# A two-layer hybrid encoder step on one core: a weight loaded two steps ahead, layer 1's parameters tied to their place, four units' weight splits moved to VectorE, and the barrier norms written in one piece

## The chip, the cores and the metric

One core of a Trainium2 chip runs the whole program. The time is the device time of one execution in microseconds (us); the kernel before takes 2740.53 us, the median of three runs (2738.47 to 2742.73). Engines are named as in the profile: PE is TensorE, DVE is VectorE, ACT is ScalarE, POOL is GpSimd, SP is the queue that issues nearly all DMAs. Each engine works off its own instructions in a fixed order and waits on semaphores.

## The reference, cut to what matters

512 prompt frames and 8 x 16 sample frames (640 columns in all) go through two layers of width 1024. Each layer computes `h = rmsnorm(x)`, `u = h @ w_in`, three branches from the columns of `u` (a convolution module, latent attention, a Mamba-2 SSD), `mix = (sum of sigmoid(gate_i) * branch_i @ w_mix_out[i]) @ w_out`, and then

```
x = x + rmsnorm(mix, g_post_mix)
f = rmsnorm(x, g_pre_ffn) @ w_gate_up
f = (silu(f[:, :D_FF]) * f[:, D_FF:]) @ w_down
x = x + rmsnorm(f, g_post_ffn)
```

So at two places in a layer (behind `w_out` and behind `w_down`) a norm of what was just computed, the residual sum and a second norm stand between one row of matmuls and the next. In the attention branch the sample frames' queries are multiplied by a transposed part of the key projection, here called `w_ukt`, before they meet the cached latents.

## The kernel before, in words

All activations lie transposed: 128 channels on the partitions, the 640 columns along the row, cut into half 0 (columns 0 to 255) and half 1 (256 to 639), `HALF`. A `Unit` is 128 output channels of one weight matrix. Its weights come in granules of four 128 x 128 blocks: `load_gran` brings one from memory on SP (tile `raw`, 4 buffers), ACT rounds it to `wh`, and DVE or POOL subtracts to get the rest, `wl` (`split`; the engine is an argument of the unit). Activations are split the same way (`hh` and `hl` for the normed input). `mm3` then does three matmuls per block: wh*hh, wh*hl, wl*hh. Products go to the tile `pg`, in PSUM, with 4 buffers, and `evac` takes them out on ACT and DVE.

The program is written by one loop at the end of `emit`, over a list of actions: run a unit's half A, run its half B, or call a hook. Loads are written three actions ahead of use (`loads[done:pos[i] + 3]`). After each half, `pump` advances side tasks: Python generators in lanes, each with a rate in steps per half. A `yield` in a task is a pause: what follows it is written at a later pump, among later matmuls. The lanes `bar` and `bar2` carry the norms, with about one step after each half of a unit with eight blocks; the lane `attn` carries attention. After this a planner (the framework's scheduler, `schedule_with_timeline_sim=True`) orders the instructions of each engine by when it believes their inputs to be there, earlier-written ones first. An instruction whose inputs it takes to be early can so be moved far ahead of where it was written.

A barrier (`barrier`, `add_halves`) is where half 0 of the next stage needs the norm of half 0 of this one. All units of the old stage run their half 0, then all of them half 1; meanwhile the norm of half 0 is advanced in lane `bar`. Then the new stage's first 12 units run half 0 (here called the A stretch), during which the norm of half 1 is advanced in lane `bar2`, and then half 1 (the B stretch). The norms are flushed where they are needed. `postnorm` (L424) sums squares over the channels with a matmul (`cs`), loads the old residual from memory (`xl`, eight DMAs), takes the root on DVE (`rsqrt`, nine short instructions, result `ry`), spreads it with a matmul (`rb`), and on DVE scales (`mo` or `dn`, eight) and adds the residual (eight); then it squares on ACT and sums on DVE (`psq`, seven adds), and stores. `prenorm` (L396) does `cs`, `rsqrt`, `rb`, scales into `ht` (eight on DVE) and splits into `hh` (ACT) and `hl` (eight on DVE). `bar_mix` (L1312) and `bar_ffn` (L1352) chain the two. The start of the kernel does the same with `first_norm`, and the end of the last layer with `bar_ffn` without `prenorm`.

`load_params` (L361) loads a layer's small parameters `pk` with a DMA on ACT's queue and derives `an` (ACT, then DVE) and `hp` (three on DVE). Layer 1's is written at the barrier between the layers. `wu` makes the units of `w_in`; in both layers POOL does their weight subtraction. In the first A and B stretch of a layer nine of the twelve units are loaded twice, once for each half; krdt, kv0, kv1 and q0 are the first four of them. `task_attn` (L621) begins with the loads of `qn` and then, four times: load `w_ukt` (`al`, 128 KB), pause, eight matmuls into `qlp`, copy, store. Convolution taps are long series of DVE instructions (`cv`) and POOL adds.

Of the kernel before, what the change touches and what calls it, by code (L numbers as in the profile page):

```python
# [13 lines left out]
AF = mybir.ActivationFunctionType  # L14
ALU = mybir.AluOpType
AX = mybir.AxisListType

D_MODEL, SEQ, DEPTH, NB, DS, PAST = 1024, 512, 2, 8, 16, 256
# [39 lines left out]
WIN_IDX = {n: i for i, n in enumerate(WIN_UNITS)}  # L58
# [13 lines left out]
BY = 2  # L72
# [4 lines left out]
def emit(tc, ctx, I, O):  # L77
    nc = tc.nc
    dma = nc.sync.dma_start
    act = nc.scalar.activation  # L80
    V, G = nc.vector, nc.gpsimd
# [16 lines left out]
    def nm(s):  # L98
        uid[0] += 1
        return f"{s}_{uid[0]}"  # L100

    def blk(shape, s="b", dt=F32):
        return bpool.tile(shape, dt, tag="b", name=nm(s))

    def hf(w, s="h", dt=F32):
        return hpool.tile([P, w], dt, tag="hf", name=nm(s))
# [7 lines left out]
    def tiny(shape, s="t", dt=F32):  # L114
        return tpool.tile(shape, dt, tag="t", name=nm(s))

    def psb(shape, s="pb"):
        return psb_.tile(shape, F32, tag="pb", name=nm(s))

    def mm(ps, l, r, a, b):  # L120
        nc.tensor.matmul(ps, l, r, start=a, stop=b)  # L121
# [14 lines left out]
    def tt(eng, o, a, b, op):  # L136
        eng.tensor_tensor(o, a, b, op=op)  # L137

    def stt(o, a, s, b, op0, op1):
        return V.scalar_tensor_tensor(o, a, s, b, op0=op0, op1=op1)  # L140
# [10 lines left out]
    def split(hi, lo, src, eng=None):  # L151
        nc.scalar.copy(hi, src)  # L152
        tt(eng or V, lo, src, hi.bitcast(F32), ALU.subtract)
# [30 lines left out]
    def colsum(sq, n):  # L184

        ps = psb([P, 24], "cs")
        for j in range(n):
            mm(ps[:, j:j + 1], sq[:, j * P:(j + 1) * P], C["ones"], True, True)
        return ps

    def rsqrt(ps, n, scale, post=1.0):

        v, q = ps[:, 8:8 + n], ps[:, 16:16 + n]
        s, r, t, y = (tiny([P, 8], x)[:, :n] for x in ("rs", "rr", "rt", "ry"))
        a = V.tensor_scalar(v, ps[:, :n], scale / post ** 2, EPS / post ** 2, op0=ALU.mult, op1=ALU.add)
        for i in tap.values():
            tc.add_manual_dep(a.ins, i.ins.name, behind)
        V.tensor_scalar(s.bitcast(I32), v.bitcast(I32), 0.5, float(0x1fbb4f2e), op0=ALU.mult, op1=ALU.add)
        V.reciprocal(r, s)
        tt(V, q, v, r, ALU.mult)  # L200
        tt(V, t, q, s, ALU.add)
        V.reciprocal(r, t)
        tt(V, q, v, r, ALU.mult)
        stt(t, t, 0.25 * HERON ** 2, q, ALU.mult, ALU.add)
        root.append(V.reciprocal(y, t))
        return y

    def bcast(y, n):
        rb = psb([P, n * P], "rb")
        for j in range(n):  # L210
            mm(rb[:, j * P:(j + 1) * P], y[:, j:j + 1].broadcast_to([P, P]), C["ident2"], True, True)
        return rb
# [144 lines left out]
    def layer(l):  # L357
# [4 lines left out]
        def load_params():  # L362
            pk = lpool.tile([P, NPK], F32, tag="pk", bufs=2, name=nm("pk"))
            nc.scalar.dma_start(pk, I["pk"][l])
            L["pk"] = pk
            an = lpool.tile([P, 16], F32, tag="an", bufs=2, name=nm("an"))
            o = _PK["a_log"][0]
            act(an, pk[:, o:o + 16], AF.Exp)
            V.tensor_scalar(an, an, -1.0, None, op0=ALU.mult)
            L["aneg"] = an  # L370
            hp = lpool.tile([P, 16], F32, tag="hp", bufs=2, name=nm("hp"))
            for j, n in enumerate(("conv_ln_g", "conv_ln_b")):
                o = _PK[n][0]
                V.tensor_scalar(hp[:, 4 * j:4 * j + 4], pk[:, o:o + 4], 0.5, None, op0=ALU.mult)
            o = _PK["d_skip"][0]
            V.tensor_scalar(hp[:, 8:16], pk[:, o:o + 8], 0.5, None, op0=ALU.mult)
            L["hp"] = hp

        def par(n, j):
            o = _PK[n][0]  # L380
            return L["pk"][:, o + j:o + j + 1]


        def new_h():
            L["h"] = [tuple(blk([P, NT], t, F32R) for t in ("hh", "hl")) for _ in range(8)]
# [4 lines left out]
        def squares(xs, half):  # L390
            r = [hf(HW[half], "psq") for _ in range(8)]
            for k in range(8):
                act(r[k], xs[k][:, HALF[half]], AF.Square)
            for a, b in ((0, 1), (2, 3), (4, 5), (6, 7), (0, 2), (4, 6), (0, 4)):
                tt(V, r[a], r[a], r[b], ALU.add)
            return r[0]  # L396

        def prenorm(xs, sq, half, gname, ps=None):
            c, w, n = HALF[half], HW[half], HCH[half]
            if ps is None:  # L400
                ps = colsum(sq, n)
            yield
            y = rsqrt(ps, n, 1.0 / D_MODEL)
            yield
            rb = bcast(y, n)
            for k in range(8):
                tmp = hf(w, "ht")
                stt(tmp, xs[k][:, c], par(gname, k), rb, ALU.mult, ALU.mult)
                hh, hl = L["h"][k]
                split(hh[:, c], hl[:, c], tmp)  # L410
            yield
# [12 lines left out]
        def postnorm(key, tiles, half, gname, src, dst, sq=True):  # L424

            c, n, w = HALF[half], HCH[half], HW[half]
            yield
            ps = colsum(L.pop(("sq", key, half)), n)
            xs = []
            for k in range(8):  # L430
                xs.append(hf(w, "xl"))
                dma(xs[k], src[k][:, c])
            yield
            rb = bcast(rsqrt(ps, n, 1.0 / D_MODEL), n)
            for k in range(8):
                t = tiles[k][:, c]
                stt(t, t, par(gname, k), rb, ALU.mult, ALU.mult)
                tt(V, t, t, xs[k], ALU.add)
            r = squares(tiles, half) if sq else None
            for k in range(8):  # L440
                dma(dst[k][:, c], tiles[k][:, c])
            for _ in range(BY):
                yield
            return r


        win = I["w_in"][l]

        def wu(name, evac, done=None):
            return Unit(win[WIN_IDX[name]], 8, h_rhs, evac, done, G)  # L450


        def ev_krdt(ps, half, c):
# [166 lines left out]
        def al(src, w, rows=P, view=None):  # L620
            t = blk([rows, w], "al") if w > 384 else hf(w, "al")[:rows]  # L621
            dma(t if view is None else view(t), src)
            return t
# [7 lines left out]
        def task_attn():  # L631
# [51 lines left out]
            for i in range(2):  # L683
                a = blk([P, 512], "qn")
                dma(a[:64].rearrange("p (h n) -> p h n", h=4), qd[4 * i:4 * i + 4, :64, SEQ:].rearrange("h p n -> p h n"))
                r.append(a)
            yield
            for ct in range(2):
                for i in range(2):
                    w = al(I["w_ukt"][l, ct, :, i * 512:(i + 1) * 512], 512, 64)  # L690
                    yield
                    ps = psb([P, 4, P], "qlp")
                    for h in range(4):
                        c = slice(h * P, (h + 1) * P)
                        mm(ps[:, h, :], w[:, c], r[i][:64, c], True, True)
                    t = blk([P, NB, 4, DS], "qlt")
                    nc.scalar.copy(t, ps.rearrange("p h (b t) -> p b h t", t=DS))
                    dma(qld[ct][:, :, i * 64:(i + 1) * 64], t.rearrange("p b h t -> p b (h t)"))
# [135 lines left out]
            for hh in range(2):  # L834
# [4 lines left out]
                for p, w in zip((2 * hh, 2 * hh + 1), uv):  # L839
                    ps = psb([P, 256], "oss")  # L840
                    o = (p % 2) * 256
# [470 lines left out]
        def bar_mix(half):  # L1312
            sq = yield from postnorm("mo", L["mo"], half, "g_post_mix", xin, xd)
            if half == 0:
                new_h()
            yield
            yield from prenorm(L["mo"], sq, half, "g_pre_ffn")


# [34 lines left out]
        def bar_ffn(half):  # L1354
            sq = yield from postnorm("dn", L["dn"], half, "g_post_ffn", xd, O["y"] if last else xd, not last)
            if not last:
                nxt = layers[l + 1]
                if half == 0:
                    nxt["load_params"]()
                    nxt["new_h"]()  # L1360
                yield
                yield from nxt["prenorm"](L["dn"], sq, half, "g_pre_mix")

        def start():
            load_params()
            new_h()
# [22 lines left out]
        def schedule():  # L1389
# [9 lines left out]
            def glu(j):  # L1399
                return [wu(f"glu{j}a", ev_glu_a(j)), wu(f"glu{j}b", ev_glu_b(j), done_glu(j))]  # L1400
# [51 lines left out]
    done = 0  # L1452
# [3 lines left out]
    for i, (k, u, half) in enumerate(actions):  # L1456
# [3 lines left out]
        if i in pos:  # L1460
            for n in loads[done:pos[i] + 3]:
                actions[n][1].load()
            done = max(done, pos[i] + 3)
# [163 lines left out]
```

## Time and profile before

| | |
|---|---|
| median of 3 runs | 2740.53 us (2738.47 to 2742.73) |
| profiled execution: time, span | 2738.25 us, 2736.4 us |
| busy: PE, DVE, ACT, POOL | 2647.6, 1557.0, 1092.8, 810.7 us |
| PE clock granted, mean | 0.988 of full speed |

The busy shares are over the whole span. The stages are different: in the projection and attention stages DVE, ACT and POOL all have much to do, in the feed-forward stages nearly only PE. Where PE has an idle gap, the profile names what ended it; the clock of a stretch is in the view of windows.

### The profile page before, as it was taken

Reading aid. Unit: us, or ns where it says so; the run is one execution under the profiler, and the core shown is the slowest. Engines: PE = TensorE matmul, PEld = TensorE weight load, DVE = VectorE, ACT = ScalarE, POOL = GpSimd, SP = SyncE. Lnnn points to the kernel's source line nnn. Section 1 sums busy time; section 2 is a strip of 40 time slices with the busy share of each in tenths; the row PEclk is TensorE's granted clock in tenths of the full one; section 3 lists DMA queues with packets and bytes.
Section 4 is the critical chain, followed back from the end, with each engine's and each line's share of the span. In section 5 each row is a group of like instructions: output and inputs, shape, how many; then the busy total and the mean of one; then the engine's idle time right before and its main releaser. Section 6 shows DMA issues by size and latency. Waiting matters only on the chain. (4 is left out here: it accounts for less than half of the span.)

```text
span 2736.4 us, 47467 instructions
## 1 busy us (share of the span) xinstructions
PE 2647.6 (97%) x17652; PEld 2556.6 (93%) x17652; DVE 1557.0 (57%) x3382; ACT 1092.8 (40%) x2437; POOL 810.7 (30%) x796
## 2 busy tenths in 40 slices
PE   7999999999999899999999899999999998999997
PEld 7999898889999899999999898989999998999997
DVE  6364759576566632333665648677656666323336
ACT  5535454434325432222445354544433344322222
POOL 5554555554420000000156544645544200000000
PEclk9999999999999999999999999999999999999999
DMA  6453244543734432222454432453436443222224
GB/s 185 147 159 102 75 135 111 156 131 119 239 121 137 149 93 74 70 82 72 139 166 158 129 98 87 128 143 120 145 110 230 133 159 120 86 77 70 78 74 131
DMA packets 248536, 337.81 MB, mean 123 GB/s; under 512 B 52464, under 2 KB 139056, under 8 KB 248304
## 3 DMA queue, kind: packets, MB, share of 16 engines
q1 hardware_dynamic: 246720, 333.75, 39.2%
q8 instruction: 139, 2.28, 0.3%
q10 hardware_dynamic: 1584, 1.02, 0.1%
q14 instruction: 93, 0.76, 0.1%
HBM read 268.73 MB, written 65.94 MB: 122 GB/s over the span
## 5 line engine op out<-in xcount | busy, mean ns | idle before, releaser
L121 PE MATMUL pg<-hh,wh 128*128 128x256 f32 (+1 forms) x3296 | 1048.4, 319 | 25.6 <-DVE fg L140 18.2
L121 PE MATMUL pg<-hl,wh 128*128 128x256 f32 (+1 forms) x3296 | 1035.1, 314 | 4.6 <-DVE hl L137 4.6
L121 PE MATMUL pg<-hh,wl 128*128 128x256 f32 (+1 forms) x3296 | 1029.2, 313 | 0.0
L137 POOL TENSOR_TENSOR wl<-raw,wh 128x512 fp32r<-128x512 f32 (+2 forms) x364 | 506.8, 1398 | 1158.5 <-ACT wh L152 1106.3
L152 ACT CAST wh<-raw 128x512 fp32r<-128x512 f32 (+1 forms) x696 | 423.7, 610 | 846.7 <-PE pg L121 737.9
L121 PEld LDWEIGHTS pg<-hh,wh 128*128 128x128 f32 x3296 | 627.3, 190 | 37.7 <-DVE fg L140 18.6
L121 PEld LDWEIGHTS pg<-hl,wh 128*128 128x128 f32 x3296 | 627.6, 191 | 13.8 <-DVE hl L137 5.3
L121 PEld LDWEIGHTS pg<-hh,wl 128*128 128x128 f32 x3296 | 627.0, 190 | 5.6 <-issue 3.9
L137 DVE TENSOR_TENSOR wl<-raw,wh 128x512 fp32r<-128x512 f32 x332 | 224.3, 677 | 338.6 <-ACT wh L152 337.0
L121 PE MATMUL pg<-fh,wh 128*128 128x256 f32 (+1 forms) x648 | 200.6, 310 | 0.0
L121 PE MATMUL pg<-fl,wh 128*128 128x256 f32 (+1 forms) x648 | 200.1, 309 | 0.0
L121 PE MATMUL pg<-fh,wl 128*128 128x256 f32 (+1 forms) x648 | 200.0, 309 | 0.0
L140 DVE SCALAR_TENSOR_TENSOR cv<-pp,pk,cv 128x512 f32<-128x512 f32 x184 | 158.8, 863 | 2.7 <-POOL cv L137 2.7
L121 PEld LDWEIGHTS pg<-fh,wh 128*128 128x128 f32 x648 | 122.0, 188 | 0.0
L121 PEld LDWEIGHTS pg<-fl,wh 128*128 128x128 f32 x648 | 122.0, 188 | 0.0
L121 PEld LDWEIGHTS pg<-fh,wl 128*128 128x128 f32 x648 | 121.9, 188 | 0.0
L140 DVE SCALAR_TENSOR_TENSOR sa<-pd,pk,sa 128x664 f32<-128x664 f32 x96 | 106.6, 1110 | 16.9 <-ACT sa L996 16.3
L137 POOL TENSOR_TENSOR cv<-cv,cvt 128x640 f32<-128x640 f32 x56 | 89.8, 1603 | 74.4 <-ACT cvt L907 66.2
L140 DVE SCALAR_TENSOR_TENSOR cv<-sp,pk,cv 128x128 f32<-128x128 f32 x184 | 94.8, 515 | 0.0
L137 DVE TENSOR_TENSOR fg<-fg,pg 128x256 f32<-128x256 f32 (+1 forms) x88 | 42.6, 486 | 83.5 <-PE pg L121 83.2
L152 ACT CAST fh<-fg 128x256 fp32r<-128x256 f32 (+1 forms) x88 | 40.3, 460 | 111.3 <-DVE fg L137 108.3
L137 DVE TENSOR_TENSOR acc<-acc,sq 128x256 f32<-128x256 f32 (+1 forms) x96 | 59.8, 625 | 37.4 <-ACT sq L421 35.9
(307 smaller groups left out, 4411.7 us busy)
## 6 DMA issues: line engine op xcount, KB each, us to landing
raw<-in_w_in SPq DMA_DIRECT2D x284, 256.0 KB, 2.9
raw<-in_w_gu SPq DMA_DIRECT2D x208, 256.0 KB, 2.7
raw<-in_w_down SPq DMA_DIRECT2D x72, 256.0 KB, 2.7
raw<-in_w_mix SPq DMA_DIRECT2D x64, 256.0 KB, 3.0
ma<-gd SPq DMA_DIRECT2D x48, 320.0 KB, 4.7
raw<-in_w_out SPq DMA_DIRECT2D x48, 256.0 KB, 2.7
gd<-gs SPq DMA_DIRECT2D x48, 192.0 KB, 2.2
hb<-in_state_ssm SPq DMA_DIRECT2D x64, 128.0 KB, 3.2
```

The lines of the kernel that those rows point to most:

```text
L121: nc.tensor.matmul(ps, l, r, start=a, stop=b)
L137: eng.tensor_tensor(o, a, b, op=op)
L140: return V.scalar_tensor_tensor(o, a, s, b, op0=op0, op1=op1)
L152: nc.scalar.copy(hi, src)
```

## The change: what it does

It changes five things. (1) `w_ukt`: the first load is written with the `qn` loads, and in each step the load for the next step but one; at any time up to two are ahead. (2) Layer 1's `an` and `hp` instructions (four on ACT and DVE) may not be moved ahead of the instruction that was written before them on their engine; their DMA may. (3) In layer 0 the weight subtraction of krdt, kv0, kv1 and q0 goes to DVE in place of POOL. (4) `prenorm` loses both its inner pauses, `postnorm` one inner pause and one of two (`BY` = 2) at its end. (5) `bar_mix` and `bar_ffn` lose the pause between the two norms.

```diff
-            act(an, pk[:, o:o + 16], AF.Exp)
+            a = act(an, pk[:, o:o + 16], AF.Exp)
+            if l:
+                tc.keep_in_program_order(a)
...
-            V.tensor_scalar(hp[:, 8:16], pk[:, o:o + 8], 0.5, None, op0=ALU.mult)
+            a = V.tensor_scalar(hp[:, 8:16], pk[:, o:o + 8], 0.5, None, op0=ALU.mult)
+            if l:
+                tc.keep_in_program_order(a)
...
-            yield
-            y = rsqrt(ps, n, 1.0 / D_MODEL)
-            yield
-            rb = bcast(y, n)
+            rb = bcast(rsqrt(ps, n, 1.0 / D_MODEL), n)
...
                 dma(xs[k], src[k][:, c])
-            yield
             rb = bcast(rsqrt(ps, n, 1.0 / D_MODEL), n)
...
-            for _ in range(BY):
-                yield
+            yield
             return r
...
-            return Unit(win[WIN_IDX[name]], 8, h_rhs, evac, done, G)
+            eng = None if l == 0 and name in ("krdt", "kv0", "kv1", "q0") else G
+            return Unit(win[WIN_IDX[name]], 8, h_rhs, evac, done, eng)
...
+            def ukt_load():
+                if len(ukt) < 4:
+                    ct, i = parts[len(ukt)]
+                    ukt.append(al(I["w_ukt"][l, ct, :, i * 512:(i + 1) * 512], 512, 64))
+
+            ukt_load()
             yield
             for ct in range(2):
                 for i in range(2):
-                    w = al(I["w_ukt"][l, ct, :, i * 512:(i + 1) * 512], 512, 64)
+                    ukt_load()
+                    w = ukt[2 * ct + i]
                     yield
...
             if half == 0:
                 new_h()
-            yield
             yield from prenorm(L["mo"], sq, half, "g_pre_ffn")
...
                     nxt["new_h"]()
-                yield
                 yield from nxt["prenorm"](L["dn"], sq, half, "g_pre_mix")
```

A unit whose engine is `None` is split on DVE.

## Rows read from the trace of the kernel before

**Rows 1.** The page, part 1: busy us, share of the span, instructions.
```profile
PE 2647.6 (97%) x17652; PEld 2556.6 (93%) x17652; DVE 1557.0 (57%) x3382; ACT 1092.8 (40%) x2437; POOL 810.7 (30%) x796
```

**Rows 2.** Waits of PE: who waited for whom, us in total, times, longest.
```profile
PE pg L121 <- DVE fg L140: 18.2, 2, 9.1
PE qlp L121 <- DMA al<-in_w_ukt: 8.7, 3, 6.2
PE rb L121 <- DVE ry L205: 8.2, 3, 3.8
...
PE pg L121 <- DVE hl L137: 4.6, 3, 1.7
```

**Rows 3.** Timeline, `w_ukt` in layer 0: start, us, engine, operation, [idle before <- releaser].
```profile
166.38 0.56 SPq L622 DMA_DIRECT2D al<-in_w_ukt  x1
169.87 2.07 PE L121 MATMUL qlp<-qn,al 64*128 64x128 f32 x8 [2.20 <-DMA al<-in_w_ukt]
```

**Rows 4.** Windows: stretch, its us, busy us by engine, PEclk (granted), DMA share, GB/s.
```profile
169.87:177.00 7.13, 7.13 (x25) 6.90 (x26) 7.13 (x15) 1.21 (x2) 0.46 (x1) 0.53 0.23 66
1536.14:1543.00 6.86, 6.86 (x26) 6.63 (x27) 2.73 (x3) 2.04 (x3) 0.59 (x4) 0.58 0.61 184
...
1364.00:1376.00 12.00, 9.59 (x48) 9.30 (x49) 7.70 (x27) 3.77 (x9) 0.47 (x2) 0.57 0.50 158
...
846.00:880.00 34.00, 34.00 (x202) 34.00 (x201) 21.65 (x61) 15.24 (x35) 0.00 (x0) 1.00 0.42 131
880.00:930.00 50.00, 39.46 (x315) 39.05 (x314) 41.87 (x101) 24.39 (x51) 0.00 (x0) 0.90 0.51 169
```

**Rows 5.** Timeline, `w_ukt` in layer 1, on POOL, SP and PE.
```profile
1516.94 14.36 POOL L137 TENSOR_TENSOR wl<-raw,wh 128x512 fp32r<-128x512 f32 x1 [4.14 <-ACT wh L152]
...
1518.67 0.61 SPq L622 DMA_DIRECT2D al<-in_w_ukt  x1
1531.33 1.60 SPq L220 DMA_DIRECT2D raw<-in_w_in  x2
...
1521.50 1.16 PE L121 MATMUL qlp<-qn,al 64*128 64x128 f32 x8 [0.23 <-DMA al<-in_w_ukt]
...
1536.14 2.04 PE L121 MATMUL qlp<-qn,al 64*128 64x128 f32 x8 [6.25 <-DMA al<-in_w_ukt]
```

**Rows 6.** Waits of SP's queue from 1500 to 1545 us.
```profile
SPq L220 <- POOL wl L137: 17.5, 4, 11.7
```

**Rows 7.** Timeline at the `w_out` barrier of layer 0, on DVE and PE.
```profile
881.62 1.42 DVE L137 TENSOR_TENSOR hl<-ht,hh 128x256 fp32r<-128x256 f32 x4
...
896.14 4.29 DVE L140 SCALAR_TENSOR_TENSOR mo<-mo,pk,rb 128x384 f32<-128x384 f32 x8 [1.91 <-PE rb L121]
...
908.99 0.74 DVE L140 SCALAR_TENSOR_TENSOR fg<-ft,pg 128x256 f32<-128x256 f32 x2
...
927.14 3.36 DVE L137 TENSOR_TENSOR hl<-ht,hh 128x384 fp32r<-128x384 f32 x7
...
909.45 0.58 PE L121 MATMUL pg<-hh,wh 128*128 128x256 f32 x1 [9.08 <-DVE fg L140]
```

**Rows 8.** Timeline of PE at the barrier between the layers.
```profile
1364.71 1.19 PE L121 MATMUL rb<-c_ident,ry 128*128 128x128 f32 x4 [2.45 <-DVE ry L205]
...
1391.92 0.58 PE L121 MATMUL pg<-hh,wh 128*128 128x256 f32 x1 [2.37 <-ACT sq L421]
```

**Rows 9.** Timeline of the start, on DVE, ACT and PE.
```profile
13.50 0.29 DVE L374 TENSOR_SCALAR hp<-pk 128x4 f32<-128x4 f32 x2 [1.66 <-DMA pk<-in_pk]
...
19.95 0.62 ACT L152 CAST wh<-raw 128x512 fp32r<-128x512 f32 x1 [1.95 <-DMA raw<-in_w_in]
...
20.62 0.58 PE L121 MATMUL pg<-hh,wh 128*128 128x256 f32 x1 [3.16 <-ACT wh L152]
```

**Rows 10.** The page, part 5: weight subtractions, busy, mean ns of one, idle before.
```profile
L137 POOL TENSOR_TENSOR wl<-raw,wh 128x512 fp32r<-128x512 f32 (+2 forms) x364 | 506.8, 1398 | 1158.5 <-ACT wh L152 1106.3
...
L137 DVE TENSOR_TENSOR wl<-raw,wh 128x512 fp32r<-128x512 f32 x332 | 224.3, 677 | 338.6 <-ACT wh L152 337.0
```

More of the change, by code (lines that the diff above doesn't have):

```diff
@@ L373, in load_params @@
                 o = _PK[n][0]
-                V.tensor_scalar(hp[:, 4 * j:4 * j + 4], pk[:, o:o + 4], 0.5, None, op0=ALU.mult)
+                a = V.tensor_scalar(hp[:, 4 * j:4 * j + 4], pk[:, o:o + 4], 0.5, None, op0=ALU.mult)
+                if l:
+                    tc.keep_in_program_order(a)
             o = _PK["d_skip"][0]
-            V.tensor_scalar(hp[:, 8:16], pk[:, o:o + 8], 0.5, None, op0=ALU.mult)
+            a = V.tensor_scalar(hp[:, 8:16], pk[:, o:o + 8], 0.5, None, op0=ALU.mult)
+            if l:
+                tc.keep_in_program_order(a)
             L["hp"] = hp
@@ L686, in task_attn @@
                 r.append(a)
+            parts = [(ct, i) for ct in range(2) for i in range(2)]
+            ukt = []
+            def ukt_load():
[3 more added lines that the diff above has]
+            ukt_load()
             yield
```

## The prediction

> **What bounds the kernel now.** I read the page's first part, then PE's waits, then for each large wait the timeline of the engines around it, and last the windows for the granted clock. PE is busy 2647.6 of 2736.4 us [rows 1], so the gap to a kernel that never stops PE is 88.8 us, and a saving counts where it lies in such a gap, or where the gap leaves PE slow. Four lines of PE's waits belong to what the change touches [rows 2]: 18.2 us in two waits at the two `w_out` barriers, 8.7 in three for `w_ukt`, 8.2 in three for the root `ry`, 4.6 in three for `hl`. Together 39.7, nearly half of the gap. The clock adds to it: after the 2.20 us wait in layer 0 [rows 3] the stretch of 7.13 us shows 0.53 of full speed, so its first part ran at 1.2 in place of 2.4 GHz [rows 4]. All sums are made against the profiled execution, 2738.25 us (span 2736.4 and 1.85 around it). The median of the runs is 2.3 higher, and I add that at the end.
>
> **`w_ukt` two steps ahead.** Layer 0: the load is issued at 166.38, PE stands still until 169.87 for 2.20 [rows 3], then computes 7.13 us at 0.53. The same work at full speed takes 7.13 x 0.53 = 3.78, so the slow clock costs 3.35. Layer 1: a first wait of 0.23, then 6.25 [rows 5], then 6.86 us at 0.58, which costs 2.9 [rows 4]. Why so long: one `wl` on POOL took 14.36 us while DVE ran convolution taps, two of SP's next `raw` loads waited for the buffers it held (SP lost up to 11.7 us in one wait [rows 6]), and the second `w_ukt` load stood behind them in SP's queue; the first, at 1518.67, had got through before [rows 5]. With the change the second load is written where the first was, so it is ahead of the blocked pair. Both price items go: 2.20 + 3.35 + 0.23 + 6.25 + 2.9 = 14.9. What is late next: the half unit behind the stalled `qlp` uses weights that PE already used for its half A, and the next unit comes one warm `qlp` (1.16 [rows 5]) and 24 matmuls later, at 34 / 202 = 0.168 each [rows 4] 4.0 us: 1529.89 + 1.16 + 4.0 = 1535.1, after the slow `wl` ended at 1531.30. So I expect no new wait. The added cost is one more buffer held for a step and no extra DMA. Bounds: -14.9, and 0 if SP's order stays.
>
> The Trainium skill ("SBUF — State Buffer", section "SBUF: two separate sides") says that GpSimd and a VectorE instruction with two SBUF inputs share a port pair as an exclusive lock, and whichever does not have it waits in full. The 14.36 us row agrees with it: 14.36 against a mean of 1.398 [rows 5, 10].
>
> **The `w_out` barriers.** Now the norm of half 0 takes about eight pumps, and its last part (`ht`, `hl`) lands on the first units of the A stretch: PE waits for `hl`, 4.6 - 1.7 = 2.9 us for both layers [rows 2]. Without the pauses it is written within the first three of the eight half-1 units. DVE has room there: 21.65 busy of 34 us [rows 4]. So the 2.9 go, and DVE enters the A stretch without the eight `hl` (two groups of 1.42) [rows 7]. The 9.08 us wait has another cause. DVE does the norm of half 1 in one run from 896.14, and the evacuation `fg` that frees a PSUM buffer is behind it, at 908.99 [rows 7]. DVE is busy 41.87 of these 50 us [rows 4], so this wait is the DVE's work, and it shrinks only by what leaves the stretch: 2.84, and a little of the `ht`. I take 3.0 of 9.08 per layer. The cost is one bunch: the second half of the norm (`ht`, as large as the 4.29 row, and `hl`, 3.36 for seven [rows 7]) follows the first at once and stands ahead of more evacuations. Together 4.3 + 3.8 = 8.1; if PE had no cover left, the wait would grow by 8.1, and if the planner slots evacuations into the gaps of the second `rsqrt`, by 0. Nearer to the second, since the second half waits for a `cs` and an `rb` on PE: I take 2 per barrier. Net: -2.9 - 6.0 + 4 = -4.9. Bounds: everything gone, -2.9 - 18.2 = -21.1; or +16.2 - 2.9 = +13.3.
>
> **The barrier between the layers.** There the units have seven blocks, a pump gives less than one step, and the norm of half 0 is not done when the matmuls are. PE waits 2.45 for `ry` [rows 8] and 1.7 for `hl`, the longest of its three waits [rows 2], and 1364 to 1376 shows 0.57 with 9.59 us busy [rows 4]: the slow clock costs 9.59 x 0.43 = 4.1. With some five pauses fewer it ends about four half units earlier (21 matmuls at 0.168, 3.5 us each), in a stretch in which PE has nothing but matmuls, so all of it goes: 8.2. The later wait of 2.37 for a square on ACT [rows 8], behind the norm of half 1, I leave, and charge 2 for the bunch as above. Net -6.2; bounds -10.6 and +8.1.
>
> **The start.** Layer 1's `hp` sits in the middle of the first root and waits 1.66 for its DMA, and takes 0.29 and a short third one [rows 9]: about 2.0 off the root. But the first units wait next for a `raw` that lands at 19.95, and PE goes on at 20.62 [rows 9]; that load is behind the `x` loads in SP's queue, which the change does not touch. What PE can gain is some work on krdt in the 3.16 us before. The four units' splits cost DVE 0.677 in place of POOL's 1.398 [rows 10], two granules each, loaded twice: 16 x 0.677 = 10.8 us more on DVE, 22.4 less on POOL. Two of them may fall into the root, 1.35 of the 2.0. The rest is covered, as PE has no wait over 0.25 us from 20.62 to the first `w_ukt`. I take -1.5 for tie and splits, bounds -5 and +2, and 2 for the bunch there (the first norm of half 1).
>
> **The sum.** 14.9 + 4.9 + 6.2 + 1.5 - 2 = 25.5; 2738.25 - 25.5 = 2712.75, and with 2.3 for the median 2715. The end of the kernel has the same chain as before, and the feed-forward stages behind the barriers are PE's alone, so a gain ahead of them stays.
>
> **Rivals.**
> A. *Only the loads count.* DVE's work at the barriers is moved but not less; 41.87 of 50 busy [rows 4] speaks for it, the low 21.65 before it and the wait for `ry` against. Then 14.9 + 1.5 = 16.4 go: 2738.25 - 16.4 + 2.3 = 2724.
> B. *The `w_ukt` loads still come late*, since the planner, not the program, orders SP, so the edit does not do what it says. For: in layer 0 the load went out only 3.5 us before its use [rows 3]. Against: it depends on nothing but a buffer. Then 25.5 - 14.9 = 10.6 go: 2730.
> C. *POOL is kept out at the layer boundary.* Layer 1's first units still split on POOL, and the residual adds, squares' sums and `hl` of one uninterrupted norm are DVE instructions with two tiles each, as the taps were at 1516.94. One such hold costs 14.36 - 1.4 = 13.0 [rows 5, 10] and one fall of the clock 3.35: 2715 + 16.4 = 2731. The Trainium skill ("SBUF — State Buffer", section "SBUF: two separate sides") would have it so. Against: at present the same instructions run there, and POOL gets through.
> D. *Slower: evacuations stand behind the whole norm.* At all four A stretches (start, two `w_out`, layer boundary) the 8.1 us of `ht` and `hl` run before the evacuations, and PE, whose PSUM buffers are already full in the 9.08 us wait [rows 7], waits 8.1 longer at each: +32.4, one more fall of the clock, 3.35, at the start. The gains without it are 14.9 + 2.9 + 8.2 + 1.5 = 27.5. So +8.2: 2738.25 + 8.2 + 2.3 = 2749. It decides from 27.5 / 4 = 6.9 us per stretch on.
>
> **How the numbers follow.** Forecast 0.55, with an own range of 2700 to 2722; A 0.16, B 0.10, C 0.07, D 0.12. A measurement of this kernel tells 0.2% (5.5 us) from no change. Faster by more: the forecast, A, a little over half of B, and C: 0.55 + 0.16 + 0.06 + 0.05 = 0.82. Within it: parts of B, C and D, 0.09. Slower: most of D, 0.09. With the good ends of the unknown costs (21.1 for the `w_out` barriers, 10.6 at the boundary, 5 at the start, 14.9) 51.6 would go, which reaches 2689; the low end 2698 leaves out what needs nearly all of them at once. The high end 2741 takes in A, B, C and leaves most of D out.
>
> **What would show it.** In the changed trace: PE's line for `w_ukt` gone and full clock behind both places; the wait for `ry` between the layers gone, and with it the 0.57; `hl` gone as a releaser; DVE's `ht` of half 0 within the old stage; the two 9.08 us waits near 6 to 8; `hp` of layer 1 near the layer boundary. I am wrong if the waits for `fg` or for `sq` grow past 15 us each, if PE waits for a `wl` of POOL in layer 1's first units, or if SP still issues the second `w_ukt` behind a blocked pair of `raw`.

## The result, and the profile after

The changed kernel takes 2760.46 us (median of 6, 2757.84 to 2766.22), the kernel before 2740.61 in the same series (2738.34 to 2742.73): 1.0076 of before, 95% interval 1.0063 to 1.0089. It is 0.8% slower, clear of the noise; the forecast was 2715, and its range ended at 2741. The profiled execution has a span of 2759.4 us, 23.0 more than before. First the page's part 1 and PE's waits of the changed kernel, which answer to [rows 1, 2]:

```profile
PE 2651.4 (96%) x17652; PEld 2559.9 (93%) x17652; DVE 1557.8 (56%) x3398; ACT 1092.6 (40%) x2437; POOL 800.7 (29%) x780
```

```profile
PE cs L121 <- DVE psq L137: 22.5, 5, 10.9
PE rb L121 <- DVE ry L205: 19.3, 11, 4.0
PE pg L121 <- DVE fg L140: 9.4, 2, 4.7
PE pg L121 <- ACT acc L421: 7.6, 2, 6.2
...
PE pg L121 <- DVE hl L137: 2.5, 1, 2.5
PE qlp L121 <- DMA al<-in_w_ukt: 2.3, 3, 1.4
```

PE does the same work with nearly the same busy time. Three of the four waits that the forecast named are smaller: `w_ukt` 8.7 to 2.3, `hl` 4.6 to 2.5, `fg` 18.2 to 9.4. But the fourth grew: `rb` waits 19.3 us for the root (8.2 before). And `cs` waits 22.5 us for the sum of squares, where the kernel before has

```profile
PE cs L121 <- DVE psq L137: 6.7, 3, 4.6
```

**The loads worked, in layer 1 above all.** SP and PE in the two layers, against [rows 3, 5]:

```profile
168.36 1.21 SPq L625 DMA_DIRECT2D al<-in_w_ukt  x2
...
1541.31 1.25 SPq L625 DMA_DIRECT2D al<-in_w_ukt  x2
1554.02 1.63 SPq L220 DMA_DIRECT2D raw<-in_w_in  x2
```

```profile
171.41 0.82 PE L121 MATMUL qlp<-qn,al 64*128 64x128 f32 x5 [1.41 <-DMA al<-in_w_ukt]
...
1544.26 1.16 PE L121 MATMUL qlp<-qn,al 64*128 64x128 f32 x8 [0.29 <-DMA al<-in_w_ukt]
1552.57 1.16 PE L121 MATMUL qlp<-qn,al 64*128 64x128 f32 x8
```

In layer 1 both first loads leave ahead of the pair of `raw` that still stands blocked until 1554.02, and the second `qlp` no longer waits. In layer 0 the two leave together, only 3 us before use, so 1.41 of 2.20 is left, and the 6.59 us behind it show 0.74 of full speed (the third number from the end):

```profile
171.41:178.00 6.59, 6.59 (x31) 6.46 (x32) 6.59 (x13) 1.21 (x2) 1.59 (x1) 0.74 0.42 127
```

**The `w_out` barrier lost.** PE and DVE in layer 0, against [rows 7], then the window of the stretch, against [rows 4]:

```profile
873.08 1.12 PE L121 MATMUL rb<-c_ident,ry 128*128 128x128 f32 x4 [1.47 <-DVE ry L205]
...
912.20 1.41 PE L121 MATMUL cs<-c_ones,psq 128*128 128x1 f32 x6 [10.06 <-DVE psq L137]
915.58 1.62 PE L121 MATMUL rb<-c_ident,ry 128*128 128x128 f32 x6 [1.97 <-DVE ry L205]
921.92 0.58 PE L121 MATMUL pg<-hh,wh 128*128 128x256 f32 x1 [4.71 <-DVE fg L140]
```

```profile
897.61 4.28 DVE L140 SCALAR_TENSOR_TENSOR mo<-mo,pk,rb 128x384 f32<-128x384 f32 x8
...
909.03 3.02 DVE L137 TENSOR_TENSOR psq<-psq,psq 128x384 f32<-128x384 f32 x6
913.64 0.17 DVE L195 TENSOR_SCALAR cs<-cs 128x3 f32<-128x3 f32 x1 [1.59 <-PE cs L121]
...
915.26 0.17 DVE L205 RECIPROCAL ry<-rt 128x3 f32<-128x3 f32 x1
917.24 4.29 DVE L140 SCALAR_TENSOR_TENSOR ht<-mo,pk,rb 128x384 f32<-128x384 f32 x8 [1.81 <-PE rb L121]
921.45 0.41 DVE L140 SCALAR_TENSOR_TENSOR fg<-ft,pg 128x256 f32<-128x256 f32 x1
921.78 3.36 DVE L137 TENSOR_TENSOR hl<-ht,hh 128x384 fp32r<-128x384 f32 x7
```

```profile
880.00:942.00 62.00, 45.26 (x336) 44.73 (x335) 47.52 (x108) 27.59 (x56) 0.00 (x0) 0.83 0.47 157
```

Before, the `fg` that PE waited for slipped in among the sums of squares at 908.99, and PE went on at 909.45. Now it comes at 921.45, behind the sums, the root and all eight `ht`, and between 902 and 921.9 PE does nothing but `cs` and `rb`. The waits add up to 10.06 + 1.97 + 4.71 = 16.74, against 9.08. The granted clock over the stretch falls from 0.90 to 0.83, and DVE is idle for 62 - 47.52 = 14.5 us of it (8.1 before). Layer 1 repeats it (10.91, 1.97, 4.71).

**The barrier between the layers lost too.** PE, against [rows 8]:

```profile
1375.49 0.68 PE L121 MATMUL rb<-c_ident,ry 128*128 128x128 f32 x4 [1.41 <-DVE ry L205]
...
1380.30 0.58 PE L121 MATMUL pg<-hl,wh 128*128 128x256 f32 x1 [2.49 <-DVE hl L137]
1404.09 0.58 PE L121 MATMUL pg<-hh,wh 128*128 128x256 f32 x1 [6.16 <-ACT acc L421]
```

**The ties did nothing.** DVE at the start, against [rows 9]:

```profile
13.45 0.16 DVE L376 TENSOR_SCALAR hp<-pk 128x4 f32<-128x4 f32 x1
13.52 0.15 DVE L137 TENSOR_TENSOR rt<-cs,rs 128x2 f32<-128x2 f32 x1
13.59 0.16 DVE L376 TENSOR_SCALAR hp<-pk 128x4 f32<-128x4 f32 x1
```

Layer 1's `hp` still sits in the first root, whose last step (`ry`) starts at 14.31, before at 14.37. By the code, each `hp` is tied behind the instruction written before it on its engine, and that is the `an` multiplication or another `hp` of the same group, which comes early along with it. That this is the reason is read from the code; no run tests it.

### The profile page after: what moved, and what is told of

Same layout as the page of the kernel before. It is cut to its first block, busy times and chain, and to the rows that moved or that the text cites. A ratio compares the mean times of both kernels' runs of the same rounds, so it can differ in the third digit from the quotient of the medians.

```text
span 2759.4 us, 47462 instructions
## 1 busy us (share of the span) xinstructions
PE 2651.4 (96%) x17652; PEld 2559.9 (93%) x17652; DVE 1557.8 (56%) x3398; ACT 1092.6 (40%) x2437; POOL 800.7 (29%) x780
## 5 line engine op out<-in xcount | busy, mean ns | idle before, releaser
L121 PE MATMUL pg<-hh,wh 128*128 128x256 f32 (+1 forms) x3296 | 1050.3, 319 | 23.6 <-DVE fg L140 9.4
L137 POOL TENSOR_TENSOR wl<-raw,wh 128x512 fp32r<-128x512 f32 (+2 forms) x352 | 500.0, 1425 | 1184.6 <-ACT wh L152 1135.1
L121 PEld LDWEIGHTS pg<-hl,wh 128*128 128x128 f32 x3296 | 628.3, 191 | 11.1 <-issue 5.1
L137 DVE TENSOR_TENSOR wl<-raw,wh 128x512 fp32r<-128x512 f32 x344 | 232.8, 678 | 352.2 <-ACT wh L152 348.1
L140 DVE SCALAR_TENSOR_TENSOR sa<-pd,pk,sa 128x664 f32<-128x664 f32 x96 | 109.0, 1136 | 10.8 <-ACT sa L1009 10.1
L121 PE MATMUL pg<-ynh,wl 128*128 128x256 f32 (+1 forms) x256 | 78.8, 309 | 0.0
```

## The experiments

The theories. **T**: PE's own order loses; `cs` and `rb`, written without pauses, stand too close in PE's queue. **D**: VectorE's order loses; the norm's second half (`ht`, `hl`) is written ahead of the evacuations `fg` of the next units and gets ahead of them on VectorE (rival D of the prediction). **B**: the buffers lose; `psq`, `ht`, `ft` and `fg` share the 11 buffers of the pool `hf`. **S**: the splits and ties lose. **R**: any edit reshuffles the planner's orders, and parts don't add up. **N**: VectorE's amount of work in the A stretch sets the end.

The table reads, from PE's timeline, when the same stages begin, and gives how much longer than before each stretch took, in us (in the changed kernel's layer 0 the A stretch runs from 883.59 to 941.69, 58.10; before from 880.12 to 929.84, 49.72; +8.38). The medians are from four series, in which the kernel before took 2740.6, 2741.5, 2742.2 and 2743.2; so medians of different series are comparable to some 3 us. "Half 0" is from the first `w_out` matmul to the A stretch; "attention" is from the end of layer 1's first B stretch to its `w_out` stage.

| kernel | half 0 at `w_out`, layer 0, 1 | A at `w_out`, layer 0, 1 | A between layers | attention, layer 1 | median us |
|---|---|---|---|---|---|
| changed | +3.3, +3.3 | +8.4, +8.6 | +12.8 | -12.5 | 2760.5 |
| e1_ukt | 0, 0 | +0.7, -0.2 | +0.5 | -12.7 | 2726.8 |
| e2_norms | +1.7, +1.8 | +9.0, +8.9 | +11.6 | -4.1 | 2776.3 |
| e3_inner | 0, 0 | +9.8, +10.3 | +4.3 | -10.4 | 2754.2 |
| e4_between | 0, 0 | +11.2, +11.4 | +4.3 | -11.6 | 2757.7 |
| e5_half1 | +1.7, +3.4 | -0.6, -2.2 | +4.5 | -9.4 | 2735.4 |
| e6_half0 | 0, 0 | +9.3, +10.1 | +8.7 | -9.6 | 2755.9 |
| e7_all | 0, 0 | +0.2, -0.2 | +0.4 | -10.2 | 2730.4 |
| g2_htlate | +1.8, +3.5 | -2.0, -2.4 | +4.9 | -8.7 | 2735.6 |
| h_after20 | +1.7, +3.5 | +8.6, +8.9 | +11.7 | -9.2 | 2766.2 |
| h_load20 | 0, +0.1 | +0.4, -0.1 | +0.1 | -6.5 | 2731.0 |
| f3_fine | 0, +0.1 | -1.5, -1.3 | +0.7 | -9.6 | 2729.8 |
| g3_nine | 0, +0.1 | +0.6, -0.2 | +0.4 | -9.7 | 2731.6 |

**The parts alone.** e1_ukt is before plus the edit of `task_attn`; e2_norms is before plus the edits of the norms' pauses; e7_all is the changed kernel with every pause back:

```diff
-            rb = bcast(rsqrt(ps, n, 1.0 / D_MODEL), n)
+            yield
+            y = rsqrt(ps, n, 1.0 / D_MODEL)
+            yield
+            rb = bcast(y, n)
...
-            yield
+            for _ in range(BY):
+                yield
             return r
```

> The kernel before with the w_ukt part alone. T (without the pauses the norms' matmuls cs and rb stand too close in PE's queue; the norms lose 34 us, the loads gain 12): the gain of the loads alone, 10.3 in layer 1 and 1.5 in layer 0, so 2740.6 - 11.8 = 2729 (2724 to 2733), PE's order at the barriers as before. R (one edit reshuffles every order, so parts do not add up): anything outside 2724 to 2733.

> The kernel before with all the pauses of the norms taken out and nothing else. T: the three barriers lose 10.7, 11.9 and 11.4, 34 in all, so 2774 (2766 to 2780). S (the four units' splits on VectorE and the ties are what costs, by other orders on VectorE): about 2741. R: between, without a term of its own at each barrier.

> The changed kernel with all pauses back: left of the change are the loads, the ties and the four units' splits. If the ties do nothing and the splits cost what they save at the start: as e1_ukt, 2727 (2723 to 2731). If the parts were worth the 1.5 of the forecast: 2725.

Measured: e1_ukt 2726.79, 0.994 of before (0.9924 to 0.9957); e2_norms 2776.28, 1.0128 (1.0109 to 1.0147); both against 2741.51. The loads give 14.7, the norms take 34.8, and 2741.51 - 14.7 + 34.8 = 2761.6, the changed kernel within 1.2. So R falls for the whole. In single stages the parts do not add up: attention in layer 1 is 12.7 shorter with the loads and 4.1 with the norms, but 12.5, not 16.8, with both. So the agreement within 1.2 is partly luck. e7_all took 2730.43 (0.9958, 0.9943 to 0.9973), and its interval overlaps that of e1_ukt: ties and splits bring nothing that can be told, and S falls. e1_ukt beats both kernels.

**Which pauses.** e3_inner puts back only the two inside `prenorm` (the first hunk above), e4_between only those between the two norms, in `postnorm` (the second hunk) and here, with the same in `bar_ffn`:

```diff
                 new_h()
+            yield
             yield from prenorm(L["mo"], sq, half, "g_pre_ffn")
```

> The changed kernel with the two pauses inside prenorm back (cs, pause, rsqrt, pause, rb); the pauses between the two norms stay out. T: at the w_out barriers PE has 32 matmuls between half 0's cs and rb in place of 2, and 22 in place of 0 in half 1, so the waits of 1.47, 1.97 and most of 10.06 go and the barriers come back to the kernel before: 2760.5 - 30 = 2730 (2723 to 2740). D (only the evacuations fg behind ht and hl on VectorE count): 4.7 and the fall of the clock behind it at each barrier go at most, 2745 to 2750. S: 2760.

> The changed kernel with the pauses between the two norms back (two more at the end of postnorm, one ahead of prenorm); cs, rsqrt and rb stay written as one. T: PE's order at the w_out barriers is the same as in e3 (32 and 22 matmuls between cs and rb), so 2730 (2723 to 2740) again, though nothing stands between cs and rb in the program. A rival T2 (what counts is that cs, rsqrt and rb are written without a pause): no gain, 2755 to 2760. S: 2760.

Measured: 2754.18 (1.004, 1.0025 to 1.0054) and 2757.65 (1.0055, 1.004 to 1.007), far from T's 2730; D's 2745 to 2750 was missed too. (By its edit e4_between has one more pause at the end of `postnorm`, two in all.) T's own condition was met: PE of e3_inner has 32 matmuls between half 0's `cs` and `rb`, and the wait of 1.47 there is gone; in half 1 it has 22, and the wait for `ry` falls from 1.97 to 0.31. The loss of half 1 stays:

```profile
914.94 0.58 PE L121 MATMUL pg<-hh,wh 128*128 128x256 f32 x1 [10.97 <-DVE fg L140]
924.15 0.91 PE L121 MATMUL rb<-c_ident,ry 128*128 128x128 f32 x6 [0.31 <-DVE ry L205]
929.77 0.58 PE L121 MATMUL pg<-hh,wh 128*128 128x256 f32 x1 [4.71 <-DVE fg L140]
```

Both kernels have four of half 1's seven pauses, in other places, and results 3.5 us apart: this speaks for their number, not their place. So T falls for half 1. e4_between lies in the range of T2, but e3_inner, with `cs`, `rsqrt` and `rb` apart, does not gain what T2 promises.

**Which half.** All pauses back in one half's norms only, half 1 (e5_half1) or half 0 (e6_half0):

```diff
-            rb = bcast(rsqrt(ps, n, 1.0 / D_MODEL), n)
+            if half == 1:
+                yield
+            y = rsqrt(ps, n, 1.0 / D_MODEL)
...
-            yield
+            for _ in range(BY if half == 1 else 1):
+                yield
             return r
```

> The changed kernel with all pauses back in the norms of half 1, none in those of half 0. D (half 1 loses because the evacuations fg, written fewer half units ahead, stand on VectorE behind the sum of squares and the eight ht; it takes all seven pauses to get them ahead): at the w_out barriers the waits for fg fall back from 10 and 4.7 to one of 9, 8.4 come back at each, 8 at the layer boundary: 2760.5 - 16.8 - 8 = 2736 (2728 to 2744). Half 0 goes on losing 3.5 at each w_out barrier by the wait of 1.5 for ry behind cs. If the loss of half 1 comes of the earlier end of half 0 (another layout of VectorE's work), 2755 or more.

> The changed kernel with all pauses back in the norms of half 0, none in those of half 1. D: half 1 keeps its loss (10 for the square sum, 2 for ry, 4.7 for fg at each w_out barrier), half 0 gives back 3.5 at each and some 4 at the layer boundary: 2760.5 - 11 = 2749 (2743 to 2756). T (cs and rb too close on PE is all): the same for half 0; so the two runs together must give back about 34, and the share of half 1 is what is asked.

Measured: 2735.44 (0.9973, 0.9963 to 0.9983) and 2755.94 (1.005, 1.0035 to 1.0065). The A stretches at `w_out` of e5_half1 are back to before, those of e6_half0 are not. Half 1 costs 2760.5 - 2735.4 = 25 us, half 0 4.5, together nearly the 30.0 that all pauses give back (2760.46 - 2730.43, e7_all). Half 0 at `w_out` gains nothing: of the three waits for `hl` in [rows 2] the two of about 1.46 at `w_out` become 1.47 for `ry`.

**Only `ht`, later.** The changed kernel with five pauses in half 1, between `rb` and `ht`:

```diff
             rb = bcast(rsqrt(ps, n, 1.0 / D_MODEL), n)
+            for _ in range(5 * half):
+                yield
             for k in range(8):
```

> The changed kernel with five pauses in half 1 between rb and the ht loop of prenorm; cs, rsqrt and rb stay one piece right behind postnorm. D (half 1 loses because ht and hl are written ahead of the next units' evacuations): the 4.7 for fg goes, one wait of about 9 to 10 is left at each w_out barrier, 8 to 9 come back at each and 4 to 8 at the layer boundary: 2760.5 - 16 - 6 = 2738 (2731 to 2744), as e5_half1. T (cs and rb written without pauses is what hurts): the waits of 10 at cs and 2 at rb stay, 2750 to 2760.

Measured: 2735.59 (0.9976, 0.9965 to 0.9986), as D says; `cs`, `rsqrt` and `rb` are written as in the changed kernel. Its DVE and PE:

```profile
911.61 1.48 DVE L137 TENSOR_TENSOR psq<-psq,psq 128x384 f32<-128x384 f32 x3
913.01 0.74 DVE L140 SCALAR_TENSOR_TENSOR fg<-ft,pg 128x256 f32<-128x256 f32 x2
913.67 1.02 DVE L137 TENSOR_TENSOR psq<-psq,psq 128x384 f32<-128x384 f32 x2
...
926.43 4.29 DVE L140 SCALAR_TENSOR_TENSOR ht<-mo,pk,rb 128x384 f32<-128x384 f32 x8 [2.13 <-PE rb L121]
```

```profile
913.48 0.58 PE L121 MATMUL pg<-hh,wh 128*128 128x256 f32 x1 [9.48 <-DVE fg L140]
```

One wait of 9.48 is left, the evacuations are back among the sums, and PE has 56 matmuls between `cs` and `rb`, though nothing was written between them: that PE had none in the changed kernel followed from the late evacuations and was not the cause.

**The buffers.** `hf` with 20 buffers in place of 11, on the changed kernel (h_after20) and on e1_ukt (h_load20):

```diff
-    bpool = pool("blk", 46)
-    hpool = pool("hf", 11)
+    bpool = pool("blk", 42)
+    hpool = pool("hf", 20)
```

> The changed kernel with 20 buffers in the pool hf in place of 11 (and 42 in blk in place of 46). B (the buffers: psq, ht, ft and fg share hf, so the tanh ft of an evacuation waits for a psq that VectorE gives back): the wait at cs falls from 10 by 3 to 5 and the 4.7 for fg goes, 7 or more at each w_out barrier, 2760.5 - 14 - 5 = 2741 or less. D (the order written on VectorE, fg behind the eight ht, which is the same with 20 buffers): the same time, 2756 to 2762.

> The kernel before with the loads, and 20 buffers in hf (42 in blk). B: the wait of 9.1 for fg at each w_out barrier falls by 3 or more, 2726.8 - 8 = 2719. D: the order on VectorE is the same, so 2727 (2723 to 2731), the wait stays at 8 to 9; fewer blk buffers may cost a little.

Measured: 2766.16 (1.0087, 1.0071 to 1.0103) and 2730.95 (0.9949, 0.9933 to 0.9966), with the wait for `fg` at 9.08 in h_load20 as it was, and 10.68, 1.97 and 4.71 at layer 0's barrier in h_after20: no gain, B falls. Both times are some 4 to 6 us above the same kernel with 11 buffers, which neither theory says (D's range ended at 2762); `blk` was smaller too, and what that costs was not measured apart. h_after20 shows the cause barest, on ACT and DVE:

```profile
911.09 0.36 ACT L1337 ACTIVATE ft<-pg 128x256 f32<-128x256 f32 x1
```

```profile
916.54 0.17 DVE L195 TENSOR_SCALAR cs<-cs 128x3 f32<-128x3 f32 x1 [1.59 <-PE cs L121]
...
920.14 4.29 DVE L140 SCALAR_TENSOR_TENSOR ht<-mo,pk,rb 128x384 f32<-128x384 f32 x8 [1.81 <-PE rb L121]
924.34 0.41 DVE L140 SCALAR_TENSOR_TENSOR fg<-ft,pg 128x256 f32<-128x256 f32 x1
```

The `ft` that the `fg` needs is done at 911.45. DVE goes on with the sums, then stands idle twice, 1.59 and 1.81 us, and does not run the 0.41 us of `fg`, for which the trace shows nothing missing (the one semaphore that it waits for is ACT's): it stands behind eight `ht` in DVE's queue until 924.34.

**Other distances.** f3_fine (on e1_ukt) moves two of half 1's pauses into the run of residual adds; g3_nine (on e1_ukt) has nine pauses in place of seven:

```diff
                 tt(V, t, t, xs[k], ALU.add)
+                if half and sq and k % 4 == 3:
+                    yield
...
-            for _ in range(BY):
+            for _ in range(0 if half and sq else BY):
                 yield
```

```diff
-            for _ in range(BY):
+            for _ in range(BY + 2 * half):
                 yield
```

> The kernel before with the loads, and in half 1's postnorm two pauses inside the run of multiplications and adds (one behind every fourth tile) in place of the two behind its end; the count of pauses stays. D: evacuations get in between the tiles, the waits of 9.08 for fg at the two w_out barriers shrink by 4 or more each: 2726.8 - 8 = 2719 (2714 to 2724). N (VectorE's work as such is the bound there, 41.9 of 50 us busy): the wait only moves, 2727 (2723 to 2732).

> The kernel before with the loads, and two pauses more between the two norms of half 1 (nine in all). D, if more distance goes on helping: the ht runs later, 2722 to 2725, with the wait of 9.1 as it is, since it stands ahead of these pauses. If seven are enough: 2727 (2723 to 2731), and if the end of the norm then comes too late for the B stretch, which in the kernel with the loads starts while the last hl run, 2730 to 2735 with waits for hl at its start.

Measured: 2729.83 (0.9957, 0.9942 to 0.9972) and 2731.56 (0.9955, 0.994 to 0.9969), neither better than e1_ukt. In f3_fine the wait for `fg` falls from 9.08 to 4.61 and 5.42, but PE waits again, 2.07 for `fg`, where the B stretch begins, and the A stretches give only 1.5 and 1.3 against before: a part of D, a part of N. In g3_nine the A stretches are as in e1_ukt, so seven pauses are enough; its time lies in its third range, but no wait for `hl` shows at the start of B, and what got longer is the B stretch between the layers, by 3.9.

## Why the prediction was wrong

The spans of the profiled executions differ by +23.0 us where the sum said -25.5. Of these 48.5 the two `w_out` barriers are 28.5 (forecast -4.9; measured 8.4 + 8.6 + 3.3 + 3.3 = +23.6) and the barrier between the layers 17.4 (forecast -6.2; measured 12.8 - 1.6 = +11.2).

- **The loads**: priced -14.9, measured -14.7 by the medians of e1_ukt (-11.0 by the two profiled spans). This match is partly luck. Layer 1's term was 9.4 (0.23 + 6.25 + 2.9); attention there is 12.7 shorter in e1_ukt and 6.5 to 12.5 in the other kernels with the loads, but e2_norms has -4.1 without them, so several us of that column are other orders. Layer 0's term was 5.55 (2.20 + 3.35), and it did not last: e1_ukt waits 1.33 with its clock full behind it and runs 3.1 ahead at the transposes (316.12 against 319.17), but then PE waits for the SSD's norm (`ry` 1.72 at 762.77, `ynh` 1.07 at 775.34), waits that before does not have, and at `w_out` it is 1.1 behind.
- **The step that failed** is the bunch of half 1: "I take 2 per barrier", between 8.1 and 0, "Nearer to the second, since the second half waits for a `cs` and an `rb` on PE". That wait does open gaps on DVE (1.59 and 1.81), but the planner's order does not put `fg` into them. So the upper end was right, 8.4 and 8.6 at `w_out`, 8.7 between the layers where half 1 alone lacks its pauses (e6_half0), and it decided the sign. That the size fits is partly luck: the 8.1 was `ht` and `hl` ahead of `fg`, but `fg` (921.45) stands behind `ht` alone, ahead of `hl` (921.78), and the rest is the root and the idle stretches on both sides of it. On PE the 8.4 are waits, 16.74 - 9.08 = 7.66, less the 1.46 for `hl` that left the stretch; `cs` and `rb` themselves took 1.41 and 1.62, at a granted clock of 0.50, the 1.2 GHz level (first line below), in place of 0.72 and 0.83 in the kernel before (second and third):

```profile
912.20:922.00 9.80, 3.12 (x13) 2.76 (x13) 6.27 (x19) 4.06 (x9) 0.00 (x0) 0.50 0.02 7
```

```profile
914.92 0.72 PE L121 MATMUL cs<-c_ones,psq 128*128 128x1 f32 x6
...
921.74 0.83 PE L121 MATMUL rb<-c_ident,ry 128*128 128x128 f32 x6
```

- **The gains of the same terms did not come.** The 6.0 off the two 9.08 waits: DVE's run of norm and sums is about as long (896.14 to 911.80 before, 897.61 to 912.05), and PE waits for it at `cs` instead (10.06). The 2.9 for `hl`: replaced by 1.47 for `ry`, a wait for which the sum had no term, and half 0 at `w_out` became 1.7 to 3.5 longer. The 8.2 between the layers rested on half 0's norm ending "about four half units earlier", 14 us: its `rb` comes 1.1 earlier in its stage (1375.49 - 1323.30 = 52.2 us from the stage's first matmul, 1364.71 - 1311.45 = 53.3 before). Half 0 there got 1.6 shorter, but the A stretch behind it 4.5 longer (e5_half1), with waits of 1.4, 1.0 and 2.1 left, and with the wait for a square on ACT, which the prediction left at its 2.37 [rows 8], at 5.50:

```profile
1396.17 0.58 PE L121 MATMUL pg<-hh,wh 128*128 128x256 f32 x1 [5.50 <-ACT sq L429]
```

- **Rival D** (chance 0.12, 2749) had the mechanism, evacuations behind the norm, and nearly the price, with the luck just named. It was still 11 short. It credited the norms with 2.9 + 8.2 = 11.1 of gains that did not come and had nothing for half 0's losses; on the other side it charged 8.1 and 3.35 at the start, where A was only 2.0 longer.
- **Rival C** happened in small and cost PE nothing that its waits show. Between the layers (1382 to 1440) POOL's 18 `wl` took 1.53 on average, 1.398 in [rows 10], and the longest 5.47 (in ns, least, median and most, in the line below). It starts at 1417.48, beside the eight `hl` of half 1's norm on DVE (1417.64 to 1421.5). In attention POOL was held again, 15.65 us for two `wl` at 1539.64 beside DVE's taps, and the loads now go around it. The Trainium skill ("SBUF — State Buffer", section "SBUF: two separate sides") calls the port pair that GpSimd and VectorE share an exclusive lock; both rows agree with it.

```profile
L137 POOL TENSOR_TENSOR wl<-raw,wh x18: 1259/1287/5473, 1386.2 to 1430.5; 128x512 fp32r<-128x512 f32 x18
```

- **Ties and splits** (-1.5): nothing that can be told; e7_all is 3.6 above e1_ukt, and the intervals overlap. The ties were without effect. The 2 for the bunch at the start was right: A there is 2.0 longer.
- **The signs of being wrong** that the prediction names did not show: the waits for `fg` are 9.4 in all and those for the squares on ACT 7.6, PE waits for no `wl`, and no `w_ukt` load that PE waits long for stands blocked. The loss came in at `cs` and `rb`, which they did not name.

Open: why the planner puts `fg` among the sums of squares when `ht`, written behind those sums in any case, is written later. That it does is shown (g2_htlate), not how. Open too is what half 0 loses between the layers: why the wait for the square on ACT grows from 2.37 to 5.50 when only half 0 lacks its pauses.

## What to carry to other kernels

A pause in a written order is a place for other work: before it is taken out, look at what it lets past on the engine that runs the long piece, here the 0.4 us evacuation without which PE stops. Written earlier is not run earlier: between the layers half 0's norm got to its `rb` 1.1 us sooner where 14 were expected. Where a cost has two ends and the choice rests on "the planner will slot it in", carry the end in which it doesn't. And a wait that moves to another line (9.08 for `fg` to 10.06 for `psq`) with the same engine busy behind it is no gain.

## What the runs showed of the hardware

An engine that stands idle does not take a ready instruction from behind a blocked one: 3.4 us of idle DVE ahead of `fg`, in h_after20. The Trainium skill ("PSUM — Partial Sum Buffer", section "Engine vs sequencer instructions") calls VectorE's queue a strict FIFO; the trace agrees. And the clock behind a short wait differed more than I had priced. After 2.20 us the next 7.13 us ran at 0.53 of the 2.4 GHz [rows 4]; after 1.41, in the changed kernel, the next 6.59 at 0.74; after 1.33, in e1_ukt, the next 7.19 at full clock:

```profile
169.81:177.00 7.19, 7.19 (x48) 7.07 (x49) 7.19 (x14) 2.27 (x5) 3.12 (x1) 1.00 0.37 122
```

The length alone does not tell: behind the same wait of 1.47 for `ry` at the `w_out` barrier, the next 48 matmuls took 0.203 us each in the changed kernel (first line, clock 0.86) and 0.177 in e5_half1 (second, 1.00).

```profile
873.85:883.59 9.74, 9.74 (x51) 9.74 (x51) 9.32 (x23) 6.27 (x15) 0.00 (x0) 0.86 0.06 22
874.76:883.26 8.50, 8.50 (x51) 8.50 (x50) 8.18 (x21) 6.15 (x15) 0.00 (x0) 1.00 0.00 0
```
